# GpSimd leaves the weight splits and the gated attention's products, and the build's scheduler gets another table of costs

## The chip, the cores and the metric

One core of a Trainium2 chip runs the whole program. The metric is the time of one execution on the device in microseconds; the times given are those of repeated runs and one execution taken with the profiler.

## What is computed

A sequence of 256 rows of 1024 numbers passes four layers, two of one kind and then two of another, all in fp32. The reference, cut to the parts that the change touches or that stand beside them:

```python
def swiglu(x, w_gate, w_up, w_down):
    return (jax.nn.silu(x @ w_gate) * (x @ w_up)) @ w_down
...
# first kind, twice: x + 0.5 ffn1, x + token_mixing, x + 0.5 ffn2; token_mixing = h @ w_in, three attentions, @ w_out
def stick_breaking_attention(q, k, v):
    ...
        z = jnp.einsum('bqhd,bkhd->bhqk', q[:, q0:kend], k[:, :kend]).astype(jnp.float32) * scale
        log_one_minus = jnp.where(strict, jax.nn.log_sigmoid(-z), 0.0)
        suffix = lax.cumsum(log_one_minus, axis=3, reverse=True) - log_one_minus
        a = jnp.where(strict, jnp.exp(log_beta + suffix), 0.0)
...
# second kind, twice: z = rms_norm(x) @ w_in, three attentions, merged by gates, @ w_out; then an MLP with squared ReLU
def gated_linear_attention(q, k, v, r, g_low, w_gate, b_gate, norm_g):
    # S_t = diag(a_t) S_(t-1) + k_t^T v_t, o_t = q_t S_t, a_t = exp(logsigmoid(g_low W + b) / tau)
    ...
        b = jnp.cumsum(ab, axis=2)
        decay = jnp.exp(jnp.where(tril[:, :, None], b[:, :, :, None, :] - b[:, :, None, :, :], -jnp.inf))
        attn = jnp.einsum('bhid,bhjd,bhijd->bhij', qb, kb, decay)
        o = attn @ vb + jnp.einsum('bhid,bhdv->bhiv', qb * jnp.exp(b), state)
```

## The kernel before, in words

**Weights.** They lie in memory as 671 blocks of 128 x 1024 fp32 numbers in the order of their use. `loads` brings each into one of three `raw` buffers by a 512 KB transfer from SyncE's queue. Each block is used as a high and a low part: `splits` makes the high part on ScalarE (a cast to fp32r into `hl[:, 0]`), then the low part, raw minus high, goes to `hl[:, 1]`. The generator `lows` makes it on VectorE in one 128 x 1024 subtraction; the generator `pooled` takes the second of two blocks that wait for it and makes it on GpSimd, in four quarters. There are six `hl` buffers. Activations are split the same way (`hl_of`, `chunk`), and a product is three matmuls: high x high, high x low, low x high.

**Stages.** ffn1, mix, ffn2 in each of the first two layers, hyb and mlp in each of the last two. In a matmul the row before its tiles tells its shape: `b<-hl,hT 128*128 128x512` contracts over 128 rows for 512 columns, `64*128` over 64 rows. Buffers: `m` and `b` in PSUM, `scr`, `mid`, `chunk`, `sts` working buffers, `hT` the normed activations turned, `tC` the gated attention's q and k.

**The mix stage.** After the q and k blocks comes a V group (`ts_group`), two groups of weight blocks whose matmuls have the weights as the moving side (`b<-hl,hT`). Between them run the three stick-breaking pairs (`att_c`): scores, Abs, Exp and Ln on ScalarE, two adds, a `tensor_tensor_scan` over 768 columns and two subtractions on VectorE, Exp on ScalarE, then transposes on TensorE (`pv_t`, `b<-ident,scr`).

**The gated attention.** `gla` works on two halves of the heads, each in two time blocks t. For each: decay matmuls (`b<-dec,sp`), Exp into `e`, the product of q and `e` on VectorE, then on GpSimd the products of k with slices of `e`: `kB` of 128 columns (t = 0 only), two slices together, four slices together. Matmuls of 64 contraction rows take them, down to blocks of 16 x 16 (`b<-scr,scr`, `b<-scr,tC`). GpSimd also raises the norms to the power -0.5 (`rstd`, `head_norm`) and scales in `nsa_pair`; both stay.

**The order.** No program order is written out. Each generator yields operations, and `Sched` simulates them while the kernel is built: `Engine.__getattr__` gives each an `Op` with a cost from a table, `ready` the time at which its operands are there, `when` the time at which its engine could take it, and `run` issues the one with the least time plus bias, `issue` then moves the engine's clock. `Sched` sets the order on every engine's queue and no time on the chip; on the chip each instruction waits for its operands. All instructions are issued in one line of `issue`, so every row reads L546.

## Time and profile before

| | |
|---|---|
| three runs | 2019.14, 2017.49, 2012.46 us (median 2017.49) |
| profiled execution | 2018.0 us, its span 2016.2 us |
| TensorE busy | 1972.2 us, 98% |
| VectorE busy | 1424.7 us, 71% |
| ScalarE busy | 1200.5 us, 60% |
| GpSimd busy | 209.1 us, 10% |
| granted TensorE clock, mean | 0.99 |

A row of the trace names line, engine, operation, tiles and shape. PE is TensorE, PEld its weight load, DVE VectorE, ACT ScalarE, POOL GpSimd. In a timeline a row begins with its start and its length in us; what stands in brackets is the idle time ahead of it and what ended that. Buffer numbers are left out. The granted clock (PEclk) is a share of full speed.

### The profile page before, as it was taken

Reading aid. Unit: us, or ns where it says so; the run is one execution under the profiler, and the core shown is the slowest. Engines: PE = TensorE matmul, PEld = TensorE weight load, DVE = VectorE, ACT = ScalarE, POOL = GpSimd, SP = SyncE. Lnnn points to the kernel's source line nnn. Section 1 sums busy time; section 2 is a strip of 40 time slices with the busy share of each in tenths; the row PEclk is TensorE's granted clock in tenths of the full one; section 3 lists DMA queues with packets and bytes.
Section 4 is the critical chain, followed back from the end, with each engine's and each line's share of the span. In section 5 each row is a group of like instructions: output and inputs, shape, how many; then the busy total and the mean of one; then the engine's idle time right before and its main releaser. Section 6 shows DMA issues by size and latency. Waiting matters only on the chain. (4 is left out here: it accounts for less than half of the span.)

```text
span 2016.2 us, 31787 instructions
## 1 busy us (share of the span) xinstructions
PE 1972.2 (98%) x11942; PEld 1729.9 (86%) x11942; DVE 1424.7 (71%) x2546; ACT 1200.5 (60%) x2321; POOL 209.1 (10%) x253
## 2 busy tenths in 40 slices
PE   8999999999999999999999999999999999999999
PEld 7888878888988887888888979998888988998887
DVE  6666977766676678876667778667667878767665
ACT  6555876655565567755556657645555655755553
POOL 1000101000100010010001132410000222410000
PEclk9999999999999998999999999999999999999999
DMA  6656344655565644456565544355555544345553
GB/s 217 227 189 209 117 152 146 219 188 190 197 215 193 204 154 153 150 169 204 191 212 174 178 147 139 124 176 179 189 188 194 178 155 139 126 137 197 189 190 124
DMA packets 100561, 353.77 MB, mean 175 GB/s; under 512 B 12435, under 2 KB 13493, under 8 KB 100406
## 3 DMA queue, kind: packets, MB, share of 16 engines
q1 hardware_dynamic: 100406, 351.74, 52.6%
q8 instruction: 93, 1.52, 0.3%
q14 instruction: 62, 0.51, 0.1%
HBM read 350.64 MB, written 1.05 MB: 174 GB/s over the span
## 5 line engine op out<-in xcount | busy, mean ns | idle before, releaser
L546 PE MATMUL m<-hT,hl 128*128 128x256 f32 (+1 forms) x5856 | 972.2, 321 | 5.3 <-DVE hT L546 3.4
L546 PEld LDWEIGHTS m<-hT,hl 128*128 128x128 f32 x5856 | 853.7, 189 | 99.9 <-DVE hT L546 4.3
L546 DVE TENSOR_TENSOR hl<-raw,hl 128x1024 fp32r<-128x1024 f32 (+1 forms) x662 | 770.5, 1169 | 201.0 <-ACT hl L546 196.8
L546 ACT CAST hl<-raw 128x1024 fp32r<-128x1024 f32 (+1 forms) x683 | 670.0, 991 | 370.7 <-PE b L546 131.3
L546 PE MATMUL b<-hl,chunk 128*128 128x512 f32 x2208 | 519.1, 391 | 0.0
L546 PEld LDWEIGHTS b<-hl,chunk 128*128 128x128 f32 x2208 | 409.1, 188 | 82.0 <-issue 1.4
L546 DVE TENSOR_TENSOR mid<-m,lo 128x256 f32<-128x256 f32 x256 | 108.5, 424 | 209.9 <-ACT lo L546 209.2
L546 PE MATMUL b<-hl,hT 128*128 128x512 f32 (+2 forms) x672 | 157.8, 383 | 9.5 <-DVE hl L546 9.0
L546 PEld LDWEIGHTS b<-hl,hT 128*128 128x128 f32 x672 | 120.6, 196 | 26.8 <-DVE hl L546 9.9
L546 ACT CAST chunk<-mid 128x256 fp32r<-128x256 f32 x152 | 61.8, 407 | 122.0 <-DVE mid L546 121.9
L546 POOL TENSOR_SCALAR scr<-scr 128x1024 f32<-128x1024 f32 x17 | 19.5, 1148 | 844.3 <-DMA scr<-ffn_post_g 453.6
L546 ACT COPY lo<-m 128x256 f32<-128x256 f32 x256 | 94.7, 370 | 15.4 <-PE m L546 15.2
L546 PE MATMUL b<-ident,scr 128*128 128x128 f32 (+2 forms) x458 | 78.5, 285 | 7.4 <-POOL scr L546 3.9
L546 PE MATMUL m<-chunk,hl 128*128 128x256 f32 x576 | 81.3, 291 | 0.0
L546 PEld LDWEIGHTS m<-chunk,hl 128*128 128x128 f32 x576 | 74.5, 195 | 1.7 <-ACT scr L546 0.7
L546 PEld LDWEIGHTS b<-ident,scr 128*128 128x128 f32 (+2 forms) x458 | 54.7, 144 | 22.3 <-DVE scr L546 8.2
L546 ACT ACTIVATE scr<-scr,sts 128x16 f32<-128x16 f32 (+2 forms) x152 | 62.8, 416 | 16.5 <-DVE sts L546 16.3
L546 DVE TENSOR_TENSOR chunk<-mid,chunk 128x256 fp32r<-128x256 f32 x152 | 64.6, 425 | 3.8 <-ACT chunk L546 3.5
L546 POOL TENSOR_SCALAR scr<-scr,sts 128x128 f32<-128x128 f32 (+2 forms) x96 | 58.1, 624 | 61.1 <-DVE sts L546 43.8
L546 POOL TENSOR_TENSOR hl<-raw,hl 128x256 fp32r<-128x256 f32 x40 | 42.3, 1080 | 210.4 <-ACT hl L546 148.1
L546 ACT COPY scr<-b 16x16 f32<-16x16 f32 (+6 forms) x148 | 34.9, 239 | 42.4 <-PE b L546 35.2
L546 ACT ACTIVATE mid<-mid 128x256 f32<-128x256 f32 x88 | 36.7, 417 | 36.7 <-DVE mid L546 36.7
(205 smaller groups left out, 1593.8 us busy)
## 6 DMA issues: line engine op xcount, KB each, us to landing
raw<-w SPq DMA_DIRECT2D x636, 512.0 KB, 3.4
scr<-mem SPq DMA_DIRECT2D x4, 512.0 KB, 7.3
scr<-ffn_post_g SPq DMA_DIRECT2D x4, 512.0 KB, 4.4
bias<-bias SPq DMA_DIRECT2D x6, 256.0 KB, 3.5
scr<-ffn_pre_g SPq DMA_DIRECT2D x3, 512.0 KB, 4.4
scr<-mem_norm SPq DMA_DIRECT2D x2, 512.0 KB, 5.3
scr<-mix_pre_g SPq DMA_DIRECT2D x2, 512.0 KB, 4.2
bias<-alibi SPq DMA_DIRECT2D x4, 256.0 KB, 3.8
```

The lines of the kernel that those rows point to most:

```text
L546: r = op.call(*op.args, **op.kw) if op.call is not None else None
```

## The change

1. `POOLED` is False: `pooled` is never started, and every low part is made by `lows` on VectorE. (The rewritten rule in `pooled` is not reached.)
2. The three products in `gla` go from `nc.gpsimd` to `nc.vector`.
3. The scheduler's table: transfers land by another formula and take 0.46 us of SyncE each, broadcast ones longer; the scan costs 2.1 ns an element instead of 1.04; powers, small ScalarE copies and matmuls cost a little more, transposes 0.098 us; a change of the contraction's row count costs TensorE 0.195 us; and operations marked `shared` on VectorE and GpSimd shut each other out.

```diff
@@ 
...
-        self.fn = fn
+        self.fn, self.mode = fn, mode
+        fast = fn in ("tensor_copy", "tensor_scalar") and not any(r[1] for r in self.ins + self.outs)
+        self.shared = eng == "pool" and fn != "memset" and kw.get("op") != OP.pow or eng == "dve" and (fast or sum(
+            not r[1] and r[5] - r[4] > 1 for r in self.ins) > 1)
 
 
 def region(a):
@@ 
             n = max(_free(a) for a in outs[:1] + ins)
             if "dma" in fn:
                 size = max(_free(a) for a in aps if a.space != bass.MemoryType.DRAM) * 4 * 128
-                return Op(e, real, args, kw, size / 360e3, outs, ins, 1.8, fn=fn)
+                wide = any(a.space == bass.MemoryType.DRAM and a.ap[0][0] == 0 and a.ap[0][1] > 1 for a in aps)
+                return Op(e, real, args, kw, size / 360e3, outs, ins, 3.4 if wide else 1.9, fn=fn)
             ps = any(a.space == bass.MemoryType.PSUM for a in outs + ins)
             tab = None
             ptr = sum(1 for a in ins if _free(a) == 1) if n > 1 else 0
             if e == "act":
                 cost = 0.833e-3 * n + (0.051 if all(a.space == bass.MemoryType.PSUM for a in ins if _free(a) > 1)
                                        else 0.093) + 0.093 * ptr + (0.09 if "accum_out" in kw else 0)
+                cost = max(cost, 0.162) + (0.045 if "accum_out" in kw else 0)
                 tab = SETS.get(args[2]) if fn == "activation" else None
             elif e == "dve":
                 fast = not ps and fn in ("tensor_copy", "tensor_scalar", "memset")
-                k = 8.3 if fn == "reciprocal" else 0.52 if fast else 1.04
+                k = 8.3 if fn == "reciprocal" else 2.1 if fn == "tensor_tensor_scan" else 0.52 if fast else 1.04
                 cost = k * 1e-3 * n + 0.068 + (0.06 if ptr else 0.0)
             else:
                 k, b = 2.07, 0.157
                 if kw.get("op") == OP.pow:
-                    k, b = 167.0, 0.3
+                    k, b = 200.0, 0.55
                 elif fn == "tensor_scalar":
                     k, b = 0.85, 0.24 if ptr else 0.15
                 elif fn == "tensor_copy":
@@ 
         self.t = {}
         self.acc = {}
         self.ver = {}
-        self.table = None
+        self.table = self.mode = None
         self.tasks = []
         self.log = None
         self.now = self.loader = 0.0
@@ 
             s += d
         return s
 
+    SWITCH = 0.195
+    STEP = 0.0105
+
     def matmul(self, op):
         w = self.ready(op)
+        if op.mode != self.mode:
+            if self.mode is not None:
+                w = max(w, self.t.get("pe", 0.0) + self.SWITCH - op.load)
+            self.mode = op.mode
         for i in range(op.passes):
             ld = max(self.loader, w) + op.load
-            self.loader = max(ld, self.t.get("pe", 0.0) + 0.002)
+            self.loader = max(ld, self.t.get("pe", 0.0) + self.STEP)
             if i == 0:
                 self.first = self.loader
             self.t["pe"] = self.stream(self.loader, op.cost, op.cols)
@@ 
     def when(self, op):
         c = self.t.get(op.eng, 0.0)
         if op.eng == "pe":
-            return max(c, max(self.loader, self.ready(op)) + op.load)
+            back = self.SWITCH if self.mode not in (None, 128) and op.mode != self.mode else 0.0
+            return max(c + back, max(self.loader, self.ready(op)) + op.load)
         s = max(c, self.ready(op))
+        if op.shared:
+            s = max(s, self.t.get("lock" + op.eng, 0.0))
         if op.tab and self.table not in op.tab and op.fn:
             s += 1.28 if op.eng == "act" else 0.0
         return s
@@ 
         if op.tab and (op.fn is None or self.table not in op.tab):
             self.table = op.tab[0]
         if op.eng == "sp":
-            self.t["sp"] = s + 0.06
-            d = max(self.t.get("dma", 0.0), s)
-            self.t["dma"] = d + op.cost
-            e = d + op.cost + op.tail
+            self.t["sp"] = s + 0.46
+            pl = self.t.get("dma", 0.0)
+            q = op.cost * 0.86
+            base = 2.05 + q + (1.5 if op.tail > 3 else 0.0)
+            e = s + base if pl - s < 1.4 else max(s + base + 0.9, pl + q)
+            self.t["dma"] = max(pl, e)
         elif op.eng == "pe":
             e = self.matmul(op)
             s = self.first
         else:
             e = s + op.cost
             self.t[op.eng] = e
+            if op.shared:
+                self.t["lockdve" if op.eng == "pool" else "lockpool"] = e
         for regs, w in ((op.ins, False), (op.outs, True)):
             for n, ps, p0, p1, lo, hi in regs:
                 l = self.acc.setdefault(n, [])
@@ 
         n, m = _free(rhs), _free(lhsT)
         wide = 2 if rhs.dtype == FT else 1
         return Op("pe", self.nc.tensor.matmul, (out,), dict(lhsT=lhsT, rhs=rhs, start=start, stop=stop, **kw),
-                  wide * 0.4167e-3 * n, [out], [lhsT, rhs], fn="mm", load=0.836e-3 * m, passes=wide,
-                  cols=wide * n * rhs.shape[0] / 128)
+                  wide * 0.4227e-3 * n + (0.0039 if n == 512 and lhsT.tensor.name.startswith("hl") else 0.0), [out], [lhsT, rhs], fn="mm", load=0.836e-3 * m + 0.011, passes=wide,
+                  cols=wide * n * rhs.shape[0] / 128, mode=rhs.shape[0])
 
     def tr(self, out, in_, k=128):
         i = self.ident[:k, :k]
-        return Op("pe", self.nc.tensor.transpose, (out, in_, i), {}, 0.8333e-3 * k, [out], [in_, i], fn="tr", load=0.107, cols=2 * k)
+        return Op("pe", self.nc.tensor.transpose, (out, in_, i), {}, 0.098, [out], [in_, i], fn="tr", load=0.109, cols=2 * k,
+                  mode=128 if k > 64 else self.sch.mode)
 
     def mm3(self, out, l, r, start=True, stop=True):
 
@@ 
             self.w[i] = t
             self.nlow += 1
 
-    POOLED = True
+    POOLED = False
     rush = False
 
     def pooled(self, low):
 
         while True:
-            yield lambda: not self.rush and len(low) > 1 or self.last_split
+            yield lambda: len(low) > (0 if self.rush else 1) or self.last_split
             if not low:
                 return
-            i, t = low.pop(1 if len(low) > 1 else 0)
+            i, t = low.pop(0 if self.rush else 1)
             raw = self.raw.pop(i)
             for o in range(0, 1024, 256):
                 s = slice(o, o + 256)
@@ 
                     yield nc.vector.tensor_copy(qF, q_[:, 0])
                 yield nc.vector.tensor_copy(q_[:, raw], q)
                 if t == 0:
-                    yield nc.gpsimd.tensor_mul(kB, e[:, 3], k)
-                yield nc.gpsimd.tensor_mul(e[:, one + 1:one + 3], e[:, one + 1:one + 3],
+                    yield nc.vector.tensor_mul(kB, e[:, 3], k)
+                yield nc.vector.tensor_mul(e[:, one + 1:one + 3], e[:, one + 1:one + 3],
                                            k[:, None, :].to_broadcast([128, 2, 128]))
-                yield nc.gpsimd.tensor_mul(e[:, 4:8], e[:, 4:8], k[:, None, :].to_broadcast([128, 4, 128]))
+                yield nc.vector.tensor_mul(e[:, 4:8], e[:, 4:8], k[:, None, :].to_broadcast([128, 4, 128]))
                 for hh in range(2):
                     r = slice(64 * hh, 64 * hh + 64)
                     A = yield self.b, 2
```

What it does to the order is shown at three places. First VectorE in the V group of the mix stage, from the second of the three stick-breaking pairs on; `hl1` is the weight block whose low part TensorE comes to next, `scr` the pairs' buffers (their numbers differ between the two builds). Before:

```order
L546 TENSOR_TENSOR scr2_74<-b3_68,scr4_76 128x384
L546 TENSOR_TENSOR scr2_74<-b0_65,scr4_76 128x384
L546 TENSOR_TENSOR mid0_102<-m1_64,lo0_106 128x256
L546 SCALAR_TENSOR_TENSOR scr1_73<-b4_69,scr3_75 128x384
L546 SCALAR_TENSOR_TENSOR scr1_73<-b5_70,scr3_75 128x384
L546 SCALAR_TENSOR_TENSOR qk5_138<-mid0_102,qk5_138 128x256
L546 TENSOR_TENSOR mid1_103<-m0_63,lo1_107 128x256
L546 SCALAR_TENSOR_TENSOR scr3_75<-rst_149,scr1_73 128x768
L546 SCALAR_TENSOR_TENSOR qk0_133<-mid1_103,qk0_133 128x256
L546 TENSOR_TENSOR scr1_73<-b4_69,scr3_75 128x384
L546 TENSOR_TENSOR scr1_73<-b5_70,scr3_75 128x384
L546 TENSOR_TENSOR hl1_97<-raw1_94,hl1_97 128x1024
```

And now:

```order
L566 SCALAR_TENSOR_TENSOR scr2_74<-b4_69,scr4_76 128x384
L566 COPY scr0_72<-b0_65 128x384
L566 SCALAR_TENSOR_TENSOR qk4_137<-mid3_105,qk4_137 128x256
L566 SCALAR_TENSOR_TENSOR scr4_76<-rst_149,scr2_74 128x768
L566 TENSOR_TENSOR hl1_97<-raw1_94,hl1_97 128x1024
L566 TENSOR_TENSOR mid0_102<-m1_64,lo0_106 128x256
L566 TENSOR_TENSOR scr2_74<-b1_66,scr4_76 128x384
L566 TENSOR_TENSOR scr2_74<-b4_69,scr4_76 128x384
L566 SCALAR_TENSOR_TENSOR qk5_138<-mid0_102,qk5_138 128x256
L566 SCALAR_TENSOR_TENSOR scr1_73<-b3_68,scr3_75 128x384
L566 SCALAR_TENSOR_TENSOR scr1_73<-b5_70,scr3_75 128x384
L566 TENSOR_TENSOR mid1_103<-m0_63,lo1_107 128x256
```

The split of `hl1` moved from behind the third pair's scan to right behind the second's.

TensorE in the same group, where `b<-ident,scr` are the transposes of those pairs and `qk` the next attention's scores. Before:

```order
L546 MATMUL b1_66<-ident_113,scr2_74 128x128 x3
L546 MATMUL b3_68<-hl0_96,hT_112 128x512 x5
L546 MATMUL b0_65<-ident_113,scr2_74 128x128 x3
L546 MATMUL b2_67<-hl1_97,hT_112 128x512 x5
L546 MATMUL b4_69<-ident_113,scr1_73 128x128 x3
L546 MATMUL b2_67<-hl1_97,hT_112 128x512
L546 MATMUL b1_66<-ident_113,scr1_73 128x128 x3
L546 MATMUL b3_68<-hl1_97,hT_112 128x512
L546 MATMUL b5_70<-qk4_137,qk3_136 128x256 x6
```

And now:

```order
L566 MATMUL b2_67<-ident_113,scr2_74 128x128 x3
L566 MATMUL b1_66<-hl0_96,hT_112 128x512 x3
L566 MATMUL b4_69<-ident_113,scr2_74 128x128 x3
L566 MATMUL b0_65<-hl1_97,hT_112 128x512 x6
L566 MATMUL b1_66<-hl1_97,hT_112 128x512 x6
L566 MATMUL b0_65<-hl2_98,hT_112 128x512 x4
L566 MATMUL b2_67<-ident_113,scr1_73 128x128 x3
L566 MATMUL b0_65<-hl2_98,hT_112 128x512
L566 MATMUL b3_68<-ident_113,scr1_73 128x128 x3
L566 MATMUL b0_65<-hl2_98,hT_112 128x512
```

The transposes of the third pair moved from between the matmuls of `hl1` to between those of `hl2`; the second pair's stay within `hl0`.

Last, VectorE in the first time block of the gated attention's second half, where `tC` holds q and k. Before, from the product of q and `e` on:

```order
L546 TENSOR_TENSOR scr2_74<-scr0_72,tC_8825 128x1024
L546 TENSOR_TENSOR scr3_75<-scr3_75,m1_64 30x256
L546 COPY scr2_74<-tC_8825 128x128
L546 TENSOR_TENSOR scr3_75<-scr3_75 30x256
L546 TENSOR_TENSOR hl0_96<-raw0_93,hl0_96 128x1024
```

And now:

```order
L566 TENSOR_TENSOR scr2_74<-scr5_77,tC_8826 128x1024
L566 TENSOR_SCALAR sts4_82<-sts4_82 128x16
L566 TENSOR_TENSOR scr1_73<-scr1_73,m1_64 30x256
L566 COPY scr2_74<-tC_8826 128x128
L566 TENSOR_TENSOR scr4_76<-scr5_77,tC_8826 128x128
L566 TENSOR_TENSOR scr5_77<-scr5_77,tC_8826 128x256
L566 TENSOR_TENSOR scr5_77<-scr5_77,tC_8826 128x512
```

The three products follow at once behind the copy, ahead of the next split. On TensorE the matmuls that take them stood, before, between those of the two `m` groups:

```order
L546 MATMUL m0_63<-chunk7_92,hl0_96 128x256
L546 MATMUL m0_63<-chunk1_86,hl0_96 128x256
L546 MATMUL m0_63<-chunk4_89,hl0_96 128x256
L546 MATMUL m0_63<-chunk2_87,hl0_96 128x256
L546 MATMUL m1_64<-chunk7_92,hl0_96 128x256 x2
L546 MATMUL m1_64<-chunk1_86,hl0_96 128x256
L546 MATMUL b0_65<-scr2_74,scr0_72 128x128
L546 MATMUL b0_65<-scr2_74,scr0_72 16x16 x4
L546 MATMUL b0_65<-scr2_74,scr0_72 32x32 x2
L546 MATMUL b0_65<-scr2_74,scr0_72 64x64
```

And now:

```order
L566 MATMUL m0_63<-hT_112,hl4_100 128x256 x24
L566 MATMUL m1_64<-hT_112,hl5_101 128x256 x6
L566 MATMUL b1_66<-scr2_74,tC_8826 128x256
L566 MATMUL b1_66<-scr2_74,scr5_77 128x128 x2
L566 MATMUL b4_69<-scr2_74,scr5_77 128x128
L566 MATMUL b4_69<-scr2_74,scr5_77 16x16 x4
L566 MATMUL b4_69<-scr2_74,scr5_77 32x32 x2
L566 MATMUL b4_69<-scr2_74,scr5_77 64x64
L566 MATMUL m1_64<-hT_112,hl5_101 128x256 x18
```

They stand together, six matmuls into a block of `m` instead of after it.

## Rows read from the trace of the kernel before

**Rows 1.** The page: busy time of each engine.

```profile
PE 1972.2 (98%) x11942; PEld 1729.9 (86%) x11942; DVE 1424.7 (71%) x2546; ACT 1200.5 (60%) x2321; POOL 209.1 (10%) x253
```

**Rows 2.** Timeline of TensorE: matmuls that waited (idle time ahead, releaser in brackets).

```profile
252.96 2.07 PE L546 MATMUL b<-hl,hT 128*128 128x512 f32 x4 [3.15 <-DVE hl L546]
...
1101.90 3.48 PE L546 MATMUL b<-hl,hT 128*128 128x354 f32 x11 [2.70 <-DVE hl L546]
...
1200.66 1.50 PE L546 MATMUL b<-scr,scr 64*128 64x128 f32 x16 [3.49 <-POOL scr L546]
...
1261.28 0.29 PE L546 MATMUL b<-ident,scr 128*48 128x128 f32 x1 [1.44 <-POOL scr L546]
```

**Rows 3.** Windows: us; busy PE, PEld, DVE, ACT, POOL; PEclk, DMA share, GB/s.

```profile
252.00:262.00 10.00, 9.04 (x31) 7.13 (x31) 6.28 (x17) 4.64 (x13) 3.17 (x2) 0.50 0.47 159
1101.70:1105.10 3.40, 3.19 (x11) 3.20 (x12) 1.89 (x3) 0.97 (x2) 3.40 (x3) 0.50 0.55 166
1200.70:1207.50 6.80, 6.80 (x43) 5.81 (x43) 2.38 (x11) 1.32 (x8) 1.95 (x3) 0.50 0.42 155
1258.00:1263.00 5.00, 3.56 (x31) 3.36 (x30) 2.73 (x3) 1.39 (x3) 5.00 (x9) 1.00 0.65 210
```

**Rows 4.** Timeline of all engines ahead of the third wait, gated attention, layer one.

```profile
1187.66 6.07 PE L546 MATMUL m<-hT,hl 128*128 128x256 f32 x48
...
1188.99 1.22 DVE L546 TENSOR_TENSOR scr<-scr,tC 128x1024 f32<-128x1024 f32 x1
...
1189.15 3.80 POOL L546 TENSOR_TENSOR sts<-sts,mhalf 128x16 f32<-128x16 f32 x1
...
1192.93 7.68 POOL L546 TENSOR_TENSOR scr<-scr,tC 128x128 f32<-128x128 f32 x3
```

**Rows 5.** Groups by form: count, busy us, mean ns, idle time before them.

```profile
L546 DVE TENSOR_TENSOR hl<-raw,hl 128x1024 fp32r<-128x1024 f32 x590 | 723.0, 1228 | 191.6 <-ACT hl L546 190.1
...
L546 DVE TENSOR_TENSOR mid<-m,lo 128x256 f32<-128x256 f32 x256 | 108.5, 424 | 209.9 <-ACT lo L546 209.2
...
L546 POOL TENSOR_TENSOR hl<-raw,hl 128x256 fp32r<-128x256 f32 x40 | 42.3, 1080 | 210.4 <-ACT hl L546 148.1 <-DVE scr L546 62.3
...
L546 POOL TENSOR_TENSOR scr<-scr,tC 128x512 f32<-128x512 f32 x8 | 18.9, 2360 | 0.0
...
L546 DVE TENSOR_TENSOR scr<-b,scr 128x512 f32<-128x512 f32 x24 | 16.5, 689 | 15.9 <-ACT scr L546 15.9
...
L546 DVE TENSOR_TENSOR_SCAN scr<-rst,scr 128x768 f32<-128x768 f32 x6 | 10.5, 1755 | 0.1
...
L546 POOL TENSOR_TENSOR scr<-scr,tC 128x256 f32<-128x256 f32 x8 | 8.1, 1006 | 43.4 <-DVE scr L546 43.4
...
L546 DVE SCALAR_TENSOR_TENSOR scr<-b,scr 128x384 f32<-128x384 f32 x12 | 6.3, 551 | 0.8 <-ACT scr L546 0.5
...
L546 POOL TENSOR_TENSOR scr<-scr,tC 128x128 f32<-128x128 f32 x4 | 3.2, 806 | 30.1 <-ACT scr L546 30.1
```

**Rows 6.** Timeline of all engines, V group of the first mix stage.

```profile
239.92 1.22 DVE L546 TENSOR_TENSOR hl<-raw,hl 128x1024 fp32r<-128x1024 f32 x1
...
245.89 1.79 PE L546 MATMUL b<-hl,hT 128*128 128x512 f32 x7
...
246.63 0.85 ACT L546 ACTIVATE scr<-scr 128x768 f32<-128x768 f32 x1 [0.44 <-DVE scr L546]
...
247.53 0.55 PE L546 MATMUL b<-ident,scr 128*128 128x128 f32 x3
...
251.41 1.50 DVE L546 TENSOR_TENSOR hl<-raw,hl 128x1024 fp32r<-128x1024 f32 x1
```

**Rows 7.** Timeline of TensorE in the gated attention: 512-column beside 64-row matmuls.

```profile
1143.54 1.20 PE L546 MATMUL b<-hl,hT 128*128 128x512 f32 x4
1144.67 0.97 PE L546 MATMUL b<-scr,scr 64*128 64x128 f32 x16
```

**Rows 8.** Windows: a stretch of the first hybrid stage, columns as in rows 3.

```profile
1150.00:1200.00 50.00, 47.17 (x329) 39.89 (x327) 41.97 (x78) 28.23 (x65) 15.90 (x10) 1.00 0.47 153
```

More of the change, by code (lines that the diff above doesn't have):

```diff
@@ L305, with __init__ @@
     __slots__ = ("eng", "call", "args", "kw", "cost", "tail", "outs", "ins", "tab", "rdy", "stamp", "fn", "load",
-                 "passes", "cols", "dep", "name")
-    def __init__(self, eng, call, args, kw, cost, outs, ins, tail=0.0, tab=None, fn=None, load=0.0, passes=1, cols=0.0):
+                 "passes", "cols", "dep", "name", "mode", "shared")
+    def __init__(self, eng, call, args, kw, cost, outs, ins, tail=0.0, tab=None, fn=None, load=0.0, passes=1, cols=0.0,
+                 mode=None):
         self.eng, self.call, self.args, self.kw, self.cost, self.tail, self.tab = eng, call, args, kw, cost, tail, tab
```

## The prediction

> **What bounds the kernel now.** I read the page first: TensorE is busy for 1972.2 us, 98% of the span, VectorE for 1424.7 and GpSimd for 209.1 [rows 1]. So no engine's total is a cause by itself. A saving can only come from two places: the 44 us in which TensorE stands still, and stretches in which it is "busy" at less than its full clock. The timeline of TensorE with waits shows the first, and the windows show the second. Four rows carry the argument [rows 2]: a wait of 3.15 us for a weight split in a mix stage, 2.70 at the start of a hybrid stage, 3.49 for GpSimd's products in the gated attention, 1.44 for GpSimd in the attention after that. The first, third and fourth come again in the second layer within 0.1 us, the second does not. Then I put windows over what follows each wait [rows 3]. After the first three the granted clock reads 0.50, the lower of its two levels (1.2 against 2.4 GHz), for 10.0, 3.4 and 6.8 us. After the 1.44 us wait it reads 1.00. Half of such a stretch is lost: 5.0, 1.7 and 3.4 us. So three waits cost 8.2, 4.4 and 6.9 us rather than 3.15, 2.70 and 3.49. In this trace waits of 2.70 us and more brought the lower clock, and one of 1.44 did not; I take no finer rule than that.
>
> **The change part by part.** The table of costs is used while the program is built; its edits cost no time themselves and work only through the order that they produce. The sum is made against the profiled execution, 2018.0 us (span 2016.2), which is 0.5 us above the median of the three runs.
>
> *G, the gated products.* For the waiting matmuls GpSimd makes three products in 7.68 us, from 1192.93 to 1200.61, and starts them only after a power of 3.80 us [rows 4]. Their factor, the product of q and e, ended on VectorE at 1190.2. After the change five VectorE instructions no longer than a 128x256 one (0.42) and the 512-wide product (0.69) [rows 5] stand behind that factor: 5 x 0.42 + 0.69 = 2.8 us, so the last product is there at about 1193.0. The order also moves: the four gated groups come directly behind six m matmuls. From TensorE's place at 1187.66 only some 30 matmuls of 6.07/48 = 0.126 us [rows 4], 3.8 us, and 1.1 us of the gated group itself lie ahead of the matmul that waited; it is reached at 1192.6. I leave a wait of 0.5 us. One place gains 3.5 - 0.5 + 3.4 = 6.4 us, and with its twin in layer two 12.8. Bounds: 0 (VectorE is late by as much) and 13.8 (no wait left).
>
> *M, the V group of the mix stage.* The wait is for the low part of block hl1. In the old order two pairs of subtractions and a scan stand ahead of this split; in the new one it follows the second scan. From the end of the split before it, 241.14 [rows 6], I count the new queue: three 256-wide of 0.42, three 384-wide of 0.55, the scan 1.755, the split 1.23 [rows 5], together 5.9 us, so the split is done at 247.0 instead of 252.9. Then the next block waits: four of 0.42, seven of 0.55, a scan and a split are 8.5 us, done at 255.5. TensorE has nine matmuls of block hl0 from 245.89 [rows 6], to 248.0. Then come transposes that need the exponential; it lies behind the split, one 256-wide and two 384-wide instructions and its own 0.85 [rows 6]: 247.0 + 0.42 + 1.10 + 0.85 = 249.4. The rest of hl0 and the twelve of hl1 are some 4.2 us, and TensorE waits again from 253.6 to 255.5. So the standing time is 1.4 + 1.9 = 3.3 us, no less than the 3.15 now; what changes is that it comes in two pieces, the first in the size of the wait after which the clock held. So I take the wait at no gain and the clock at 5.0 us in each of two mix stages: **-10.0**. Bounds: 0 (the lower clock comes all the same) and -16.4 (both pieces hidden).
>
> *E, the start of the first hybrid stage.* There the split moves ahead of a reduction of 1.2 us. Of the 2.70 us wait 1.2 go, what stays is near 1.44, and the 1.7 of clock go with it: **-2.9**; bounds 0 and -4.4.
>
> *S, changes of the contraction's row count.* The new table charges for them, and the order has 53 in place of 93. Sixteen 128x512 and 64-row matmuls interleaved show the price: four 512-wide ones end 1.13 us after their start where the next row begins [rows 7], against 1.64 for seven in the mix stage [rows 6], 0.234 each, so 0.94: 0.19 too much for two changes, 0.1 for one. 40 x 0.1 = **-4.0**; bounds 0 and -7.6, if one change bears all 0.19.
>
> *D, what VectorE takes over.* Ten weight splits (40 pieces of a quarter each) at 1.23 are 12.3 us; the twenty products at 0.69 (eight), 0.42 (eight) and, scaled down between these two widths, 0.29 (four) are 10.1 [rows 5]. Together 22.4 us, in an engine that idles for 8 of 50 us even in the densest hybrid stretch [rows 8]. Most is covered by that idle time; where it isn't, a split comes late. Nothing in the trace shows this price. Below it is 0; above it is the whole 22.4. Of the ends the first is nearer, since TensorE waits for VectorE only where a queue of several us has formed; but mix and hybrid stages have such queues. I take one more wait of the 1.44 kind in each of the four attention stages: **+5.6**.
>
> A rule of the Trainium skill speaks against this part. Its page "Perfetto Trace Analysis", in the section "Optimizing Scalar/DVE Operations", says that with a saturated VectorE moving operations to another engine, even GpSimd, may make sense, though the two share a read port, so that moving between them might not help. By it the moved work would cost up to its full 22.4 us; it is the second rival below. The trace has both halves of it: VectorE idle 8 of 50 us [rows 8], and a split beside a GpSimd split at 1.50 against 1.23 [rows 5, 6].
> On G, the page "GPSIMD Engine Reference", section "4.1 Engine selection", puts a two-input elementwise operation on GpSimd at about twice VectorE's time. By that the three products would take an estimated 2.8 us, no wait would exist and G would be 0, with 2007 us for the whole; the rows give 2360 ns against 689 at 512 columns [rows 5], 3.4 times, and 7.68 us for the three [rows 4], and they decide.
>
> The sum: 2018.0 - 12.8 - 10.0 - 2.9 - 4.0 + 5.6 = 1993.9, so **1994 us**.
>
> **The rivals.**
> *1. The lower clock stays in the mix stages.* The standing time there does not shrink, it is only split, and no row shows two waits of 1.4 and 1.9 close together. Then M is 0: 2004 us. For it: my second piece of 1.9 lies between 1.44 and 2.70. Chance 0.22.
> *2. VectorE becomes the late engine (slower).* The 22.4 us fall into stages where it is already the densest: a queue that grows by 3 us in front of a split makes a wait like the mix stage's. It decides from the point where TensorE waits 2.7 us or more in one piece: each such wait costs 8.2 us at the mix stage's price. With none of G, M, E gained (the waits pass from GpSimd to VectorE) and one new such wait in each of the two hybrid stages: 2018 - 4 + 16.4 = 2030 us. For it: 42 of 50 us busy. Against it: the new queue behind the gated factor is counted above, 2.8 us for what takes GpSimd 7.68, and it ends in time. Chance 0.08.
> *3. The change does not do what it says.* The table describes durations better, but the order it gives trades one wait for another: G's 12.8 are gained, new waits and a lower clock elsewhere take them back to within 6 us. About 2012 us. Chance 0.12.
> *4. More than the sum.* No new waits (D 0) and half of M's waits gone as well: 1993.9 - 5.6 - 3.2 - 4 (switches at the upper price) = 1981 us. Chance 0.10.
>
> **How the numbers follow.** The forecast case has 0.48 and runs from 1986 (D at 0, some of M's standing time hidden) to 1999 (D doubled). 0.3% of the time, some 6 us, is about what a measurement of this kernel tells from no change: the line is 2011. Rivals 1 and 4 and the forecast are faster: 0.48 + 0.22 + 0.10 = 0.80. Rival 3 is the same, 0.12, rival 2 slower, 0.08. The range takes in rival 1 with room for new waits, and about half of rival 4: 1981 to 2010; outside are rivals 2, 3 in part, and the rest of 4.
>
> **What would show it.** Right: no GpSimd product in the gated attention, no wait of 3.5 us there in either layer, the clock at 1.00 in the 7 us behind it; two shorter waits for splits in the V group instead of one, at full clock; VectorE at about 1447 us. Wrong in M: clock 0.50 for 10 us in a mix stage. Wrong in D: waits of 2.7 us or more for a split in new places, above all in the hybrid stages. Wrong altogether: TensorE's idle time unchanged with the same number of half-clock stretches.

## The result, and the profile after

The changed kernel takes 1987.88 us (median of four runs, 1985.56 to 1990.43) against 2016.37: ratio 0.986, 95% interval 0.9839 to 0.9882. That is 28.5 us less; forecast were 24, and the time lies inside the range of 1981 to 2010. The profiled execution's span fell from 2016.2 to 1988.3 us, by 27.9.

The page after, busy time of each engine:

```profile
PE 1955.8 (98%) x11942; PEld 1717.8 (86%) x11942; DVE 1422.1 (72%) x2582; ACT 1200.1 (60%) x2327; POOL 139.0 (7%) x193
```

Against [rows 1], TensorE is busy 16.4 us less for the same 11942 matmuls, and idle for 32.5 us instead of 44.0. VectorE took over work that the prediction put at 22.4 us, and is busy 2.6 us less than before.

Where it went is seen in windows over the two mix stages, the start of the first hybrid stage, and the gated attention and the attention after it in layers one and two of the hybrid kind. Columns as in [rows 3]. The windows after begin and end where TensorE has begun as many matmuls as at the ends of the windows before, since the changed kernel is 6 us ahead by 300 us and 30 by 1690. Before:

```profile
190.00:300.00 110.00, 105.84 (x631) 90.31 (x630) 89.89 (x198) 81.69 (x184) 13.32 (x15) 0.95 0.41 137
720.00:830.00 110.00, 105.86 (x633) 90.37 (x631) 90.44 (x199) 81.86 (x184) 13.32 (x15) 0.95 0.42 140
1060.00:1150.00 90.00, 87.10 (x609) 82.17 (x608) 68.66 (x111) 57.12 (x110) 13.39 (x13) 0.98 0.53 176
1150.00:1225.00 75.00, 71.51 (x523) 61.95 (x521) 59.70 (x118) 40.49 (x94) 22.36 (x17) 0.95 0.45 149
1225.00:1300.00 75.00, 73.15 (x608) 70.27 (x608) 59.55 (x201) 56.43 (x179) 25.66 (x47) 1.00 0.37 126
1620.00:1690.00 70.00, 66.48 (x472) 57.89 (x472) 54.94 (x109) 39.55 (x93) 21.85 (x16) 0.95 0.47 156
1690.00:1765.00 75.00, 73.15 (x611) 69.65 (x610) 59.96 (x200) 55.00 (x177) 26.06 (x48) 1.00 0.40 127
```

After:

```profile
190.20:294.20 104.00, 99.95 (x632) 84.90 (x631) 89.97 (x202) 80.80 (x184) 5.12 (x6) 1.00 0.44 142
714.10:818.60 104.50, 101.32 (x634) 86.39 (x633) 90.78 (x203) 81.02 (x183) 4.74 (x6) 0.98 0.43 142
1048.80:1133.70 84.90, 84.20 (x611) 79.59 (x612) 69.22 (x116) 55.56 (x110) 6.81 (x6) 1.00 0.58 186
1133.70:1205.30 71.60, 70.44 (x527) 62.14 (x526) 60.59 (x127) 43.04 (x103) 12.56 (x5) 0.98 0.51 162
1205.30:1278.70 73.40, 72.67 (x608) 70.11 (x608) 58.36 (x186) 52.67 (x159) 20.72 (x45) 1.00 0.41 134
1596.20:1659.80 63.60, 62.26 (x472) 54.76 (x471) 55.69 (x113) 38.67 (x92) 6.86 (x5) 1.00 0.49 158
1659.80:1735.50 75.70, 73.80 (x612) 70.87 (x610) 60.46 (x192) 54.78 (x161) 21.48 (x42) 1.00 0.43 140
```

The seven windows last 605.0 us before and 577.7 after: they hold 27.3 of the 27.9 us. Now read TensorE's idle time (length less busy time) and the clock. First mix stage: 4.2 us idle before and 4.1 after, but the clock goes from 0.95 to 1.00. Second: 4.1 to 3.2, 0.95 to 0.98. Start of the hybrid stage: 2.9 idle to 0.7, 0.98 to 1.00. The gated attention: 3.5 to 1.2 and 3.5 to 1.3, 0.95 to 0.98 and 1.00. The attention after it: 1.9 to 0.7, and 1.9 in both kernels in the second layer, clock 1.00 throughout. The low stretches that are left in the body, with one more window beside them:

```profile
794.60:798.00 3.40, 3.40 (x12) 2.28 (x12) 2.39 (x12) 3.40 (x12) 0.00 (x0) 0.50 0.45 159
1187.20:1190.50 3.30, 3.30 (x21) 3.08 (x19) 3.23 (x6) 0.45 (x3) 0.00 (x0) 0.50 0.62 195
1805.00:1808.30 3.30, 3.28 (x15) 3.28 (x16) 3.04 (x5) 0.90 (x2) 0.00 (x0) 0.50 0.53 180
271.00:274.40 3.40, 3.37 (x22) 2.49 (x22) 2.42 (x13) 3.05 (x11) 0.00 (x0) 1.00 0.50 159
```

Three stretches of some 3.4 us stand where five of 3.4 to 10.2 us stood; the last row is told at the end.

VectorE and TensorE around the V group of the first mix stage, after:

```profile
245.87 1.20 DVE L566 TENSOR_TENSOR hl<-raw,hl 128x1024 fp32r<-128x1024 f32 x1
...
249.85 1.74 DVE L566 TENSOR_TENSOR_SCAN scr<-rst,scr 128x768 f32<-128x768 f32 x1
...
253.23 3.48 DVE L566 TENSOR_TENSOR hl<-raw,hl 128x1024 fp32r<-128x1024 f32 x3
```

```profile
237.06 2.12 PE L566 MATMUL m<-hT,hl 128*128 128x512 f32 x8 [1.03 <-DVE mid L566]
...
247.82 2.26 PE L566 MATMUL b<-hl,hT 128*128 128x512 f32 x9
...
251.19 4.26 PE L566 MATMUL b<-hl,hT 128*128 128x512 f32 x16
```

The split of hl1 ends at 247.07 us, where the prediction counted 247.0; the next one at 254.4 (a third of the row of three), counted at 255.5. TensorE begins the group at 247.82, 1.9 us later than before [rows 6], after a wait of 1.03 us at 237.06 and with the next scores taken first. The group then runs without a wait; the two shorter ones that were forecast inside it did not come.

The gated attention of layer one, after:

```profile
1173.01 1.22 DVE L566 TENSOR_TENSOR scr<-scr,tC 128x1024 f32<-128x1024 f32 x1
...
1174.68 1.21 DVE L566 TENSOR_TENSOR scr<-scr,tC 128x128 f32<-128x128 f32 x3
```

```profile
1176.57 1.31 PE L566 MATMUL b<-scr,scr 64*128 64x128 f32 x20
...
1185.80 0.30 PE L566 MATMUL b<-ident,scr 30*128 30x30 f32 x2 [1.16 <-DVE scr L566]
```

The three products take 1.21 us on VectorE, back to back, against 7.68 on GpSimd [rows 4], and end 1.7 us after the product of q and e; 2.8 were counted. No matmul waits for them. A new wait of 1.16 us stands at 1185.80, for a chain of short operations on VectorE and ScalarE.

### The profile page after: what moved, and what is told of

Same layout as the page of the kernel before. It is cut to its first block, busy times and chain, and to the rows that moved or that the text cites. A ratio compares the mean times of both kernels' runs of the same rounds, so it can differ in the third digit from the quotient of the medians.

```text
span 1988.3 us, 31753 instructions
## 1 busy us (share of the span) xinstructions
PE 1955.8 (98%) x11942; PEld 1717.8 (86%) x11942; DVE 1422.1 (72%) x2582; ACT 1200.1 (60%) x2327; POOL 139.0 (7%) x193
## 5 line engine op out<-in xcount | busy, mean ns | idle before, releaser
L566 DVE TENSOR_TENSOR hl<-raw,hl 128x1024 fp32r<-128x1024 f32 (+1 forms) x678 | 779.1, 1155 | 188.9 <-ACT hl L566 178.9
L566 PE MATMUL b<-hl,hT 128*128 128x512 f32 (+2 forms) x672 | 148.6, 370 | 0.7 <-DVE hT L566 0.4
L566 PEld LDWEIGHTS b<-hl,hT 128*128 128x128 f32 x672 | 116.1, 188 | 17.8 <-DVE hl L566 1.5
L566 POOL TENSOR_SCALAR scr<-scr 128x1024 f32<-128x1024 f32 x17 | 23.8, 1397 | 915.9 <-DMA scr<-ffn_post_g 299.7
L566 PE MATMUL b<-ident,scr 128*128 128x128 f32 (+3 forms) x458 | 78.0, 284 | 8.4 <-DVE scr L566 6.8
L566 PEld LDWEIGHTS b<-ident,scr 128*128 128x128 f32 (+3 forms) x458 | 53.4, 143 | 22.5 <-DVE scr L566 13.4
L566 ACT ACTIVATE scr<-scr,sts 128x16 f32<-128x16 f32 (+2 forms) x152 | 62.9, 417 | 16.5 <-DVE sts L566 16.4
L566 PE MATMUL b<-hT,hl 128*128 128x256 f32 x384 | 49.3, 283 | 3.0 <-ACT hl L566 3.0
L566 POOL TENSOR_TENSOR sts<-sts,mhalf 128x4 f32<-128x4 f32 (+3 forms) x16 | 33.3, 2082 | 262.9 <-DVE sts L566 262.9
L566 POOL TENSOR_SCALAR scr<-scr,sts 128x128 f32<-128x128 f32 (+1 forms) x96 | 44.6, 487 | 93.0 <-DVE sts L566 79.0
```

The source lines that it names most:

```text
L566: r = op.call(*op.args, **op.kw) if op.call is not None else None
```

## The experiments

The change has three parts: the products (P), the splits (S) and the table (T). Six runs beside it take them apart; ratios are to runs of the kernel before at the same time. Where the changed kernel lets GpSimd split, its rewritten rule in `pooled` is reached, so T in table_only and after_pooled is the table with that rule.

| parts | run | median us | ratio, 95% interval |
|---|---|---|---|
| P | muls_only | 2004.28 | 0.9939 [0.9924, 0.9954] |
| S | nopool_only | 2013.05 | 0.9998 [0.9987, 1.0009] |
| T | table_only | 2009.67 | 0.9963 [0.9949, 0.9977] |
| P + S | oldtable_both | 1988.26 | 0.9854 [0.9839, 0.9870] |
| T + S | after_gpmuls | 2000.82 | 0.9914 [0.9900, 0.9929] |
| T + P | after_pooled | 2001.68 | 0.9945 [0.9926, 0.9965] |
| P + S + T | the change | 1987.88 | 0.9860 [0.9839, 0.9882] |

**muls_only.** The kernel before with

```diff
-                    yield nc.gpsimd.tensor_mul(kB, e[:, 3], k)
+                    yield nc.vector.tensor_mul(kB, e[:, 3], k)
...
```

and so for the other two products.

> The kernel before with the three gated products on VectorE, old table, GpSimd still splitting. Theory A (each long wait costs its idle time plus half of the low-clock stretch behind it, and the table repairs the mix stage): the two waits of 3.5 us for GpSimd's products and their two 6.8 us stretches at 0.50 go, the mix stage's two waits of 3.15 us with their 10.2 us at 0.50 stay; 93 row-count changes become 85, 0.8 us: 2016 - 12.8 - 0.8 = 2003 us. Theory B (the products on GpSimd were cover, the new order of the table brings the gain): 2013 to 2018 us. Theory C (any new order shuffles waits): no fixed place keeps its wait, and the mix stage's wait changes too.

Measured 2004.28 us, theory A's figure. The mix stage keeps its wait (timeline of TensorE):

```profile
252.95 1.20 PE L546 MATMUL b<-hl,hT 128*128 128x512 f32 x4 [3.14 <-DVE hl L546]
```

and its low clock, 6.8 us long instead of 10.2. The wait for the products is gone in both layers. Theories B and C fall for this part. The low clock did not go with the wait altogether: from 1150 to 1225 us TensorE does not stand at all, and the window still holds 3.4 us at 0.50, which makes its mean 0.98:

```profile
1150.00:1225.00 75.00, 75.00 (x556) 66.41 (x557) 61.33 (x134) 44.59 (x105) 11.90 (x10) 0.98 0.49 159
```

**oldtable_both.** Both moves, and not one number of the table:

```diff
-    POOLED = True
+    POOLED = False
...
-                    yield nc.gpsimd.tensor_mul(kB, e[:, 3], k)
+                    yield nc.vector.tensor_mul(kB, e[:, 3], k)
...
```

> Both moves from GpSimd to VectorE with the old table: the whole change but for the scheduler's numbers. Theory A: as with the products alone, 2003 us, plus 0 to 3 us where VectorE's ten splits are not hidden; the mix stage keeps 3.15 us of wait and 10.2 us at 0.50. Theory B: 2013 to 2018 us, since the table is missing. Theory D (GpSimd's splits disturbed VectorE): below 2001 us.

Measured 1988.26 us: neither A nor B. The figure is in D's range. The gain shows in TensorE's waits and clock; whether a VectorE that GpSimd disturbs less has a share in it, as D says, this run does not separate (GpSimd does disturb it, as the last section shows). Windows at the times used for the kernel before (first mix stage, the three of the first hybrid layer):

```profile
190.00:300.00 110.00, 108.24 (x667) 93.45 (x667) 95.73 (x218) 86.45 (x197) 5.13 (x8) 0.98 0.46 147
1060.00:1150.00 90.00, 87.85 (x624) 81.40 (x624) 68.71 (x112) 55.48 (x107) 4.21 (x2) 1.00 0.58 192
1150.00:1225.00 75.00, 74.75 (x594) 67.53 (x594) 65.65 (x154) 48.34 (x123) 8.58 (x7) 1.00 0.46 153
1225.00:1300.00 75.00, 74.68 (x622) 72.16 (x621) 55.29 (x172) 52.04 (x151) 27.79 (x51) 1.00 0.40 135
```

The mix stage loses only 1.8 us to idle time and the clock is 0.98. With the products moved, taking the splits off GpSimd is worth 16 us, and the whole gain needs no new table.

**table_only.** The changed kernel with `POOLED = True` and the products on `nc.gpsimd`.

> The new table and the rewritten rule of the pooled splits, with the splits and the products on GpSimd. Theory A: the mix stage's wait and clock mend (-9.6 as in the changed kernel) and the start of the first hybrid stage (-3.9), 16 fewer row-count changes at 0.09 (-1.4), while GpSimd's products still make TensorE wait twice with 6.8 us at 0.50: 2016 - 15 = 2001 us. Theory B: within 3 us of the changed kernel, 1985 to 1991 us.

Measured 2009.67 us, 8 less than before; A's 2001 was too low, B is out. The low clock did leave the mix stages, as A said, and GpSimd's products are waited for in both layers. But GpSimd now makes 22 splits instead of 10 (88 quarters in the trace against the 40 of [rows 5]), and many waits near 1 us came.

**after_gpmuls.** The changed kernel with the products back on GpSimd.

> The changed kernel with the three products back on GpSimd and nothing else. Theory A: two waits of about 3.5 us and two 6.8 us stretches at 0.50 come back (+13.8), 77 row-count changes instead of 53 (+2.2): 1988 + 16 = 2004 us. Theory B: 1988 to 1991 us. Since the new table prices GpSimd's products about as the old, the scheduler may hide part of them: between 1995 and 2004 would be A with a smaller wait.

Measured 2000.82 us, 13 more than the change by the medians, 11 by the ratios: A with a smaller wait. The row of TensorE:

```profile
1182.88 1.22 PE L566 MATMUL b<-scr,scr 64*128 64x128 f32 x4 [2.47 <-POOL scr L566]
```

It is 2.47 us, not 3.5, with 10.2 us of low clock behind it in layer one and 6.8 in layer two. So a wait for the products costs some 5.5 to 6.5 us a place here too.

**nopool_only.** The kernel before with `POOLED = False` alone.

> The kernel before with no weight split on GpSimd, the products still there, old table. The two moves together gave 2017.5 - 1988.3 = 29.2 us, the products alone 13.2, and in that run the mix stage kept its wait of 3.14 us. Theory A2 (taking the splits off GpSimd is what mends the mix stage, by the order it gives VectorE, and the two moves add up): 2017.5 - 16 = 2001 us, no low clock in the V group of the mix stage, GpSimd's products still waited for in two places. Theory C (only both moves together give the good order): 2008 to 2018 us. My own forecast before this took the splits' move as a cost of 0 to 5.6 us: 2018 to 2023 us.

Measured a ratio of 0.9998: A2's sum is refuted, and C is right in its figure. The profile shows that A2 holds for the mix stages and that another stage takes it back (windows of the two mix stages and of the attention after the products, both layers; TensorE's waits in the last):

```profile
190.00:300.00 110.00, 107.69 (x669) 92.76 (x669) 95.81 (x217) 85.94 (x197) 5.12 (x8) 1.00 0.46 147
720.00:830.00 110.00, 108.27 (x668) 93.39 (x667) 96.52 (x224) 85.72 (x196) 5.14 (x8) 0.98 0.46 151
1225.00:1300.00 75.00, 69.65 (x565) 66.40 (x564) 53.97 (x186) 51.26 (x159) 27.44 (x52) 0.98 0.34 112
1690.00:1765.00 75.00, 69.90 (x568) 66.16 (x568) 56.17 (x191) 52.44 (x172) 26.12 (x52) 0.95 0.35 112
```

```profile
1241.16 0.84 PE L546 MATMUL m<-chunk,hl 128*128 128x256 f32 x2 [2.21 <-ACT chunk L546]
1243.79 0.29 PE L546 MATMUL b<-ident,scr 128*48 128x128 f32 x1 [1.79 <-POOL scr L546]
```

The mix stages stand for 2.3 and 1.7 us at 1.00 and 0.98, much as in oldtable_both, and the products are waited for, 2.02 us in each layer. But in the stretch from 1225 TensorE is busy for 69.65 of 75 us against 73.15 before, and from 1690 for 69.90, at 0.98 and 0.95: it waits for ScalarE's chunk and for GpSimd's scaling. With the products on VectorE the first of these stretches reads 74.68 at 1.00 (above). On the old table the splits' move gains only with the products' move, which alone gives 12 us. On the new table it gains without it: after_gpmuls is 9 to 10 us below table_only, though there 22 splits leave GpSimd and not ten.

**after_pooled.** The changed kernel with `POOLED = True`.

> The changed kernel with GpSimd splitting again (by the rewritten rule). Theory A2: the table alone took the low clock out of the mix stage too (2009.7 us with both on GpSimd) but left many waits near 1 us; with the products moved as well 2009.7 - 13 = 1997 us. Theory C2 (GpSimd's splits only disturb the products): 1985 to 1990 us, no different from the changed kernel. A third way, VectorE's twelve us of splits mattered: below 1983 us.

Measured 2001.68 us, 14 more than the change by the medians, 17 by the ratios; C2 and the third way fall, A2 is off by 5. Its profile has the least low clock of the four with T, one stretch of 3.4 us in the body, and yet 42.9 us of idle TensorE (32.5 in the change): the price of these splits is waits, not clock.

**after_oldscan.** The changed kernel with

```diff
-                k = 8.3 if fn == "reciprocal" else 2.1 if fn == "tensor_tensor_scan" else 0.52 if fast else 1.04
+                k = 8.3 if fn == "reciprocal" else 0.52 if fast else 1.04
```

> The changed kernel with the scan at the old 1.04 ns an element in the table. In this order the split of the block hl1 stands behind the third scan again, as in the kernel before. Theory of my prediction (that place makes the wait and the low clock): +8 to +10 us, 1996 to 1998 us, a wait near 3 us in both V groups. Theory A2 (with no split on GpSimd, the queue ahead is another one and TensorE comes later): 1986 to 1991 us.

Measured 1989.17 us, no slower than the change beyond the spread of the runs. The split of hl1 and TensorE in the V group, and the window of the stage:

```profile
250.97 1.21 DVE L566 TENSOR_TENSOR hl<-raw,hl 128x1024 fp32r<-128x1024 f32 x1
```

```profile
249.13 2.26 PE L566 MATMUL b<-hl,hT 128*128 128x512 f32 x9
252.04 0.55 PE L566 MATMUL b<-ident,scr 128*128 128x128 f32 x3 [0.66 <-ACT scr L566]
```

```profile
190.00:300.00 110.00, 104.86 (x656) 89.25 (x655) 94.69 (x215) 85.00 (x191) 5.31 (x7) 1.00 0.45 147
```

The split ends at 252.2, almost as late as before (252.9), but TensorE begins the group at 249.13 instead of 245.89. It stands for 5.1 us in the stage, more than the 4.2 before, in many pieces (the one inside the group is 0.66 us), and the clock is 1.00. So the place of this split, on which term M rested, is not what mended the stage: with the split as late as that, no wait of 3 us came and the clock held. Why it held is not shown.

**old_switch.** oldtable_both and, of the table, only the charge `SWITCH = 0.195` for a change of the row count.

> Both moves with the old table, to which only the charge for a change of the row count is added: 53 such changes instead of 81 with the old table alone (1988.3 us). At 0.09 us each, as the steps between matmuls of unlike rows in the profile of the changed kernel give it: 1988.3 - 2.5 = 1985.8 us. If the charge's new order makes other waits: 1988 to 1992 us. If one change costs nothing: 1988 us.

Measured 1988.90 us: no gain in time from 28 fewer changes. By the two pages TensorE is busy for 3.9 us less than in oldtable_both (1954.3 against 1958.2) and idle for 7.8 us more (35.4 against 27.6); it waits 2.1 us ahead of a transpose in each mix stage, where oldtable_both has no wait over 1.2. That is the expectation's second case. What a change costs is not shown: its price and the new waits may cancel here.

**after_again.** The changed kernel, a second profile.

> The changed kernel once more, unchanged: which of its waits and low-clock stretches come at the same place in a second profiled execution. Theory A (each is fixed by the order): 3.4 us at 0.50 again at about 795, 1187 and 1805 us, the same waits within 0.2 us, 1986 to 1990 us. Theory E (a wait near 1 us decides nothing by itself, the start of the stretches shifts between executions): the waits the same, the low-clock stretches elsewhere or fewer.

Measured 1986.96 us, neither A nor E wholly: the stretches at 1187 and 1805 came again, the one at 795 did not. Most waits repeat within 0.5 us at the same matmul, but not all: the one of 1.34 us at 1636 is gone, and one of 1.16 us stands at 1641.9, at a matmul that had none. So the order alone does not fix the waits either.

**after_more_dve.** The changed kernel with

```diff
                 yield self.nc.vector.tensor_sub(t[:, 1, s], raw[:, s], t[:, 0, s].bitcast(FT))
+                if i % 8 == 4:
+                    yield self.nc.vector.tensor_sub(t[:, 1, s], raw[:, s], t[:, 0, s].bitcast(FT))
```

> The changed kernel with every eighth block's low part made twice on VectorE (the same numbers again): 84 x 1.23 = 103 us more of VectorE, 1422 to 1525 us. By the price that my prediction took for moved work, 5.6 us for 22.4 us moved, one quarter: +26 us, 2014 us. Theory A3 (the idle time of VectorE takes it, since the splits run ahead of TensorE by several blocks): +0 to +6 us, 1988 to 1994 us. Theory of the second rival (VectorE is the late engine already): +50 us and more.

Measured 1991.24 us, 4.3 more than after_again, A3's case. The page:

```profile
PE 1954.0 (98%) x11942; PEld 1713.9 (86%) x11942; DVE 1510.1 (76%) x2663; ACT 1199.8 (60%) x2325; POOL 136.6 (7%) x193
```

VectorE is busy for 88.8 us more than in after_again (1421.3), where 103 were expected, and the time grows by 0.05 us for each.

**two_tables.** The old table orders the first two layers, the new one (old scan) the last two; both moves are in.

```diff
+LATE = [False]
...
+                    k, b = (200.0, 0.55) if LATE[0] else (167.0, 0.3)
...
+        LATE[0] = True
```

and so at every number of the table; the last line stands in `setup2`.

> Both moves; the old table orders the first two layers, the new one (with the old scan price) the last two. By stages, from the profiles: old table and both moves leave 1.8 and 1.7 us of idle TensorE in the two mix stages against 4.0 and 3.2 in the changed kernel; the new one with the old scan leaves 0.9 us in the last two layers' attention up to the products against 2.8 and has 57 row-count changes in place of the old table's 81. If the halves keep their waits: 1988 - 1.5 to 4 us = 1984 to 1986.5 us, idle TensorE below 24 us. If the second half's waits depend on how the first ends: 1987 to 1990 us.

Measured 1986.31 us against 1986.96 for after_again: no difference that can be told. The mix stages stand for 2.0 and 1.7 us as hoped, the gated attention for 2.6 in each layer, not 0.7 and 0.9 as in after_oldscan. TensorE is idle for 31.1 us, not below 24: the halves did not keep their waits, and the figure near the expected one is no support for it. No version beat the changed kernel by more than the spread of the runs.

## Why the prediction was right, and where it was not

The sum was right by its main line: three kinds of waits with the low clock behind them go, and that is most of the gain. By the windows, the mix stages gained 1.1 us of idle time and, by half the length of their low stretches (10.2 and 10.2 to none and 3.4), 8.5 of clock; the two gated attentions 4.5 and 5.1, the attentions behind them 1.1, the start of the hybrid stage 2.2 and 1.7: 24.2 of 27.9. The other 3.7 are not assigned. That 24.1 were forecast is in part luck: G was taken too large, E too small, S is not borne out, D was priced as a loss, and these errors nearly cancel.

- **G**, forecast -12.8: the mechanism is shown by muls_only (-12.3 by its ratio) and after_gpmuls (+12.9 by the medians, +11 by the ratios). In the change itself the place gives 9.6, since a new wait of 1.16 us with 3.4 us of low clock stands in layer one, and one of 1.34 us in layer two. The prediction took the mean of 2360 ns for GpSimd's pace at 512 columns; that mean mixes two cases, told at the end.
- **M**, forecast -10.0: measured -9.6. The size and the time of the split (to 0.1 us) were right; the way to the size was not. No wait stands in the V group, where 1.4 and 1.9 us were counted. That the stage stands for 4.1 us as before is chance: waits elsewhere make it up (0.61 us at 229, 1.03 at 237, 1.03 at 271). And "the split moves ahead of the third scan" is not needed (after_oldscan). The wait of 3.15 us and its low clock leave the V group by the splits' move on the old table (nopool_only), and by the new table while GpSimd splits more than before (table_only). The step in the scheduler that does it was not traced, and how far GpSimd's work beside VectorE's has a part in it stays open.
- **E**, forecast -2.9: measured -3.9, since no wait over 0.5 us is left there where 1.5 was counted. It is no sure gain of both moves: in oldtable_both 2.15 us of wait stay there, without low clock behind them.
- **S**, forecast -4.0: not borne out as a term of its own, and not refuted. old_switch has the 53 changes, 3.9 us less of busy time, and no gain.
- **D**, forecast +5.6, is a term that was mis-sized. I priced each moved microsecond on VectorE at a quarter; after_more_dve gives 0.05, by which 22 us would cost an estimated 1. The moved work did not add to VectorE's busy time either: 1447 us were named as a sign, 1422 were measured. The new waits near 1 us are there, as forecast, but the attention after the products did not lose; it gained 1.1 us, which no term held.
- **Rival 1** and **rival 2** did not come; of the first, one stretch of 3.4 us in the second mix stage is left in one of two profiles. The second would have needed a VectorE without slack; 88.8 us more of work cost 4.3. **Rival 3** has a true core that I did not see: the table alone trades waits (table_only, -0.4%), and on top of both moves it adds nothing that can be measured. With one move alone it is not neutral: it takes the splits' move from 0.9998 to 0.9914 (after_gpmuls).

The rule of the Trainium skill against which the prediction was weighed ("Perfetto Trace Analysis", section "Optimizing Scalar/DVE Operations") speaks of a saturated VectorE; at 71% busy it was not one. after_more_dve shows the same from the other side.

## What to carry to other kernels

Price a wait of the engine that bounds the kernel with what the clock does behind it: here 3 us of waiting cost 6 to 8 where the low clock stood behind them, and it did not always. When an edit moves work and a build-time scheduler reorders everything, test the parts one at a time and in pairs: here, on the old table, one part was worth 12 us, another 0, both 29, and the new table of costs nothing on top. And try load on the engine that takes the work before fearing it.

## What the runs showed that I had not expected

**The low clock does not follow the wait's length.** I took from the trace that 2.70 us and more brought it and 1.44 did not. That was too much already for that trace: a wait of 3.26 us at its start, 3.3 us, has 1.00 behind it. In the changed kernel the same wait ahead of the same matmuls stands in both mix stages, 1.03 us at 271 and 1.07 at 794; the window behind the second reads 0.50, behind the first 1.00 (the last of the four windows above). In the second profile the wait at 270.6 was 1.16 us, without low clock (window of after_again, with the one at 1184 beside it):

```profile
270.60:274.00 3.40, 3.39 (x22) 2.49 (x22) 2.42 (x13) 3.07 (x11) 0.00 (x0) 1.00 0.43 159
1183.80:1187.00 3.20, 3.20 (x20) 2.83 (x18) 3.13 (x7) 0.18 (x2) 0.00 (x0) 0.50 0.73 230
```

And in oldtable_both 3.4 us at 0.50 begin at 269.4 us though TensorE had no wait over 0.3 us since 236; in the 2 us before, it did matmuls that contract over 32 rows:

```profile
267.55 1.32 PE L546 MATMUL b<-qk,qk 32*128 32x256 f32 x12
```

```profile
269.40:272.80 3.40, 3.40 (x11) 2.66 (x10) 3.36 (x22) 2.61 (x12) 0.00 (x0) 0.50 0.78 265
```

So a low stretch needs no wait ahead of it, and what the engine works on may matter as the waits do. No run tests that; what decides was not found.

**Work on GpSimd made VectorE's own instructions longer.** Groups by form, of the kernel before and of the changed one:

```profile
L546 DVE SCALAR_TENSOR_TENSOR chunk<-hlk,chunk 128x256 fp32r<-128x256 f32 x16 | 9.4, 608 | 1.3 <-ACT chunk L546 1.0
...
L546 DVE COPY scr<-tC 128x128 f32<-128x128 f32 x8 | 4.9, 608 | 0.2
```

```profile
L566 DVE SCALAR_TENSOR_TENSOR chunk<-hlk,chunk 128x256 fp32r<-128x256 f32 x16 | 6.4, 418 | 1.0 <-ACT chunk L566 1.0
...
L566 DVE COPY scr<-tC 128x128 f32<-128x128 f32 x8 | 1.8, 226 | 0.2
```

Same shapes and counts, 608 to 418 ns and 608 to 226. The timeline of the kernel before shows one of the long copies:

```profile
1220.12 2.03 POOL L546 TENSOR_TENSOR scr<-scr,tC 128x256 f32<-128x256 f32 x2 [5.67 <-DVE scr L546]
...
1221.03 1.35 DVE L546 COPY scr<-tC 128x128 f32<-128x128 f32 x1
```

GpSimd's products end at 1222.15, the copy at 1222.38, which is 0.23 us later: as long as a copy takes now. It stood still until GpSimd was done. Over the whole trace, the VectorE instructions whose form comes equally often in both kernels are 16.7 us shorter in sum after the change; so most of the work that VectorE took over was made good. The Trainium skill has a rule for it on its page "SBUF — State Buffer", section "SBUF: two separate sides": the port pair that the two engines share is "an exclusive lock, not a bandwidth split". The trace agrees: the copy ended when GpSimd's products had, plus its own 0.23 us.

**VectorE's work made GpSimd's products longer, too.** Of the eight 512-wide products in the kernel before, six took 1.28 to 1.30 us, and two took 5.58, at the two places where TensorE waited 3.5 us. One of each, and the last VectorE row beside the long one:

```profile
1195.03 5.58 POOL L546 TENSOR_TENSOR scr<-scr,tC 128x512 f32<-128x512 f32 x1
```

```profile
1220.87 1.28 POOL L546 TENSOR_TENSOR scr<-scr,tC 128x512 f32<-128x512 f32 x1
```

```profile
1198.27 1.20 DVE L546 TENSOR_TENSOR hl<-raw,hl 128x1024 fp32r<-128x1024 f32 x1
```

VectorE works without a pause on two-input instructions until 1199.47, and the product ends 1.14 us later, at 1200.61. So the wait came not from GpSimd's own pace alone: 1.28 us is 1.9 times VectorE's 0.69, and the 3.4 times of the prediction is the mean of both cases. In after_gpmuls the three products took 8.8 us at this place again. That they would have been in time without VectorE's work beside them is not shown; no run tests it.
